# VectorE takes over the sums and low parts of the stored hidden blocks in a two-layer decoder

## The chip, the core and the metric

The kernel runs on one core of one Trainium2 chip. The metric is the time of one execution on the device, in microseconds; every time below is in that unit unless it says ns. The kernel before takes 2506.91 (median of three runs, 2505.78 to 2507.61).

A core has five engines, each with an instruction queue of its own that it works off in order: TensorE (PE; its weight loads are PEld), VectorE (DVE), ScalarE (ACT), GpSimd (POOL) and SyncE (SP). SP issues most loads, ACT the stores spoken of here. Engines wait for each other by semaphores.

## The reference

Two decoder layers over x of 1024 x 1024 (sequence by channels), all in float32. The part that the change touches is the first half of the feed-forward layer:

```python
def swiglu_ffn(x, w_gate, w_up, w_down):
    return (jax.nn.silu(x @ w_gate) * (x @ w_up)) @ w_down

for l in range(DEPTH):
    ...                       # mixer, cross-attention over memory, each with a LayerNorm
    y = swiglu_ffn(x, ffn_wg[l], ffn_wu[l], ffn_wd[l])
    x = layer_norm(ALPHA * x + y, ln_ffn_g[l], ln_ffn_b[l])
```

The hidden width is 2816, so x @ w_gate and x @ w_up are products of 1024 x 1024 by 1024 x 2816, and the last one is 1024 x 2816 by 2816 x 1024.

## The kernel before

**Products.** A float32 number is split into a high part (rounded to float32r) and a low part (the rest, also as float32r). A product of two such numbers is three matmuls of 128 x 128 by 128 x 512: low by high, high by low, high by high (lines 210 to 212). A large matrix product is made with seven block products in the place of eight (Strassen's scheme in Winograd's form): sums of blocks of both sides are formed first, and the results are added afterwards.

**The gate and up stage** (function ffn). The hidden columns are 22 blocks of 128; block c and block c + 11 form a pair, and so do the two halves of the sequence. For each c from 1 to 10 there are two steps m: an even m for the gate weights and an odd one for the up weights. Each step is seven block products, in the order 1, 2, 6, 5, 7, 3, 4 (ORDER_P); each product is 4 x 3 = 12 matmuls into a bank of PSUM named P. That is 140 products in a layer. c = 0 is done without the scheme ahead of them (plain, banks named pl).

Products 1, 6, 7 and 4 run one after another in one bank, 5 and 3 in a second, 2 in a third. After products 1, 6 and 5 ScalarE copies the bank to a tile u (line 1296); only then may the next product of that bank begin. After products 2, 7, 3 and 4 the result is finished (finish): for the gate VectorE adds u to the bank (line 1199) and ScalarE takes the SiLU (line 1200; product 4 directly from the bank, line 1197); for the up part VectorE adds (1206) and multiplies by the gate (1207; product 4 at once, 1204). The result lies in tiles hf.

**The weights' operands** (operands, operand). For each product a block of weights, or a sum of blocks, is split: ScalarE casts the high part (line 1112), VectorE subtracts for the low part (line 1113). The sums are s1 (line 1130), s2 (1133), a11 - a21 (1136) and a12 - s2 (1139), all on VectorE. Operands are made three products ahead: while product n is put in the queue, the operand of n + 3 is.

**The stored blocks** (store). When the four tiles of a block c are finished, its sums and differences s1 to s4 are made, each is split, and high and low parts go to DRAM (hD), from where the down stage loads them as its operands. GpSimd makes the four sums (lines 1180 to 1185) and the low parts (1167, 1171); ScalarE makes the high parts (1166, 1170) and issues the stores (1174). These steps are put in a list, later, each with a number of products to wait; emit_later, called once in each product, behind the product's matmuls and ahead of its copy or finish, puts those that are due into the queues.

**The down stage** (ffn_down) follows without a break; its products run in banks D. VectorE sums blocks of the down weights (line 777) and splits them (lines 215 and 216), and VectorE and GpSimd multiply and add a row of gains and offsets to the residual x (lines 1366 and 1367).

All of these tiles but the weights as loaded (raw, four buffers) lie in one pool of 44 pages; a page that comes free is given to a later tile, which waits for the page's last user.

## Time and profile before

| | |
|---|---|
| median of three runs | 2506.91 |
| the profiled execution | 2508.21 |
| its span, first to last instruction | 2506.4 |
| mean granted clock of TensorE | 0.974 |
| busy: PE / PEld | 2325.8 (93%) / 1916.3 (76%) |
| busy: DVE / ACT / POOL | 1826.7 (73%) / 1049.4 (42%) / 1027.0 (41%) |

The shares are of the whole span. Matmuls overlap in the pipeline, so the duration of one (some 395 ns) is longer than the distance from one to the next. In a timeline a row is one instruction, or several of a kind without idle time between them, with its start and duration; the bracket at its end is the idle time of the engine just before it and what ended that. A group's row gives the count, the busy time, the mean duration in ns, and the idle time before its instructions. P, D, u, op, hf, s, sh, x and wp in such rows are the tiles named above (sh: a high part on its way to DRAM; sg: a gate; op: an operand of weights).

### The profile page before, as it was taken

The numbers are of one execution on the slowest core, as the hardware profiler recorded it, in microseconds if no ns is written. First come the engines' busy times: TensorE is split into PE (matmuls) and PEld (weight loads), VectorE is DVE, ScalarE is ACT, GpSimd is POOL, SyncE is SP. The second block draws the span as 40 slices with busy tenths as digits, with TensorE's granted clock in tenths as the row PEclk, the third lists the DMA queues.
The fourth block names the chain that finished last, engine by engine and source line by source line (L and its number), as shares of the span: only waits on it lengthen the run. The fifth ranks groups of instructions, "written<-read, shape, count | busy, mean of one in ns | idle before, by whom it ended". The sixth has DMA issues, their size and how long they took to land. (4 is left out here: it accounts for less than half of the span.)

```text
span 2506.4 us, 29564 instructions
## 1 busy us (share of the span) xinstructions
PE 2325.8 (93%) x11208; PEld 1916.3 (76%) x11208; DVE 1826.7 (73%) x1950; ACT 1049.4 (42%) x1727; POOL 1027.0 (41%) x577
## 2 busy tenths in 40 slices
PE   8999997798979999999999989797999999999997
PEld 7777776696868777777778789686787777777886
DVE  6986788787895777777784556879666767677555
ACT  3254554354637443434312244455563434342212
POOL 1333446666472434343530074656523525255001
PEclk9999998898989999999999999899999999999999
DMA  4211133150212243434786642302114344349773
GB/s 181 67 34 35 34 118 126 34 185 17 88 39 93 101 160 118 167 111 173 280 339 238 228 152 97 106 18 109 51 57 171 120 157 138 140 160 357 292 282 118
DMA packets 117341, 344.02 MB, mean 137 GB/s; under 512 B 10832, under 2 KB 11344, under 8 KB 117200
## 3 DMA queue, kind: packets, MB, share of 16 engines
q1 hardware_dynamic: 70560, 244.35, 28.0%
q10 hardware_dynamic: 46640, 97.79, 10.3%
q8 instruction: 89, 1.46, 0.2%
q14 instruction: 52, 0.43, 0.1%
HBM read 239.34 MB, written 102.76 MB: 136 GB/s over the span
## 5 line engine op out<-in xcount | busy, mean ns | idle before, releaser
L210 PE MATMUL P<-xh,op 128*128 128x512 f32 x1120 | 442.6, 395 | 40.4 <-ACT u L1296 37.7
L211 PE MATMUL P<-xl,op 128*128 128x512 f32 x1120 | 438.7, 392 | 0.0
L212 PE MATMUL P<-xh,op 128*128 128x512 f32 x1120 | 438.5, 392 | 0.0
L1113 DVE TENSOR_TENSOR op<-raw,op 128x512 fp32r<-128x512 f32 x200 | 231.0, 1158 | 154.6 <-ACT op L1112 103.3
L210 PEld LDWEIGHTS P<-xh,op 128*128 128x128 f32 x1120 | 211.8, 189 | 99.0 <-ACT u L1296 47.0
L210 PE MATMUL D<-dh,dl 128*128 128x512 f32 x560 | 226.0, 404 | 58.3 <-DVE x L247 35.4
L210 PE MATMUL D<-dh,wp 128*128 128x512 f32 x616 | 241.6, 392 | 10.4 <-ACT dh L215 9.2
L1180 POOL TENSOR_TENSOR s<-hf,hf 128x512 f32<-128x512 f32 x22 | 34.8, 1584 | 524.6 <-DVE hf L1207 439.3
L211 PE MATMUL D<-dl,wp 128*128 128x512 f32 x616 | 241.8, 392 | 5.2 <-DVE dl L216 5.1
L212 PEld LDWEIGHTS P<-xh,op 128*128 128x128 f32 x1120 | 211.8, 189 | 45.0
L211 PEld LDWEIGHTS P<-xl,op 128*128 128x128 f32 x1120 | 211.7, 189 | 43.1
L211 PE MATMUL D<-dl,dh 128*128 128x512 f32 x560 | 224.5, 401 | 21.1 <-DVE dl L216 21.1
L212 PE MATMUL D<-dh,wp 128*128 128x512 f32 x616 | 240.7, 391 | 0.0
L125 POOL TENSOR_TENSOR wl<-raw,wh 128x1024 fp32r<-128x1024 f32 x64 | 172.4, 2705 | 166.0 <-ACT wh L123 165.7
L216 DVE TENSOR_TENSOR dl<-wp,dh 128x1024 fp32r<-128x1024 f32 x96 | 142.5, 1493 | 117.8 <-ACT dh L215 75.6
L212 PE MATMUL D<-dh,dh 128*128 128x512 f32 x560 | 223.5, 399 | 0.0
L257 POOL TENSOR_SCALAR lst<-lst 128x1 f32<-128x1 f32 x48 | 27.3, 568 | 460.2 <-ACT sq L256 459.8
L215 ACT CAST dh<-wp 128x1024 fp32r<-128x1024 f32 x96 | 93.7, 989 | 266.5 <-DVE wp L777 68.6
L365 DVE SCALAR_TENSOR_TENSOR cacc<-sig,par,cacc 128x1023 f32<-128x1023 f32 (+14 forms) x120 | 175.6, 1464 | 2.5
L210 PEld LDWEIGHTS D<-dh,dl 128*128 128x128 f32 x560 | 108.9, 195 | 85.4 <-issue 36.6
L1112 ACT CAST op<-raw 128x512 fp32r<-128x512 f32 x200 | 121.9, 620 | 104.6 <-DVE raw L1139 73.2
L216 POOL TENSOR_TENSOR dl<-xf,dh 128x1024 fp32r<-128x1024 f32 x48 | 141.5, 2964 | 39.6 <-ACT dh L215 29.2
(272 smaller groups left out, 5498.2 us busy)
## 6 DMA issues: line engine op xcount, KB each, us to landing
wp<-hD SPq DMA_DIRECT2D x140, 512.0 KB, 5.8
hD<-sh ACTq DMA_DIRECT2D x66, 512.0 KB, 5.2
raw<-in_wg SPq DMA_DIRECT2D x44, 512.0 KB, 4.4
raw<-in_wu SPq DMA_DIRECT2D x44, 512.0 KB, 3.8
hD<-hf ACTq DMA_DIRECT2D x44, 512.0 KB, 5.8
hD<-s ACTq DMA_DIRECT2D x44, 512.0 KB, 3.6
wp<-in_wd SPq DMA_DIRECT2D x40, 512.0 KB, 7.7
xD<-x ACTq DMA_DIRECT2D x32, 512.0 KB, 3.8
```

The source lines that it names most:

```text
L125: eng.tensor_tensor(lo, raw, hi.bitcast(F32), op=ALU.subtract)
L210: mm(out, ll, rh, start=start, stop=False, skip_group_check=more)
L211: mm(out, lh, rl, start=False, stop=False, skip_group_check=more)
L212: mm(out, lh, rh, start=False, stop=stop, skip_group_check=more)
L215: self.nc.scalar.copy(hi, src)
L216: getattr(self.nc, lo_engine).tensor_tensor(lo, src, hi.bitcast(F32), op=ALU.subtract)
L257: nc.gpsimd.tensor_scalar(st[:, 3:4], st[:, 3:4], 1.0 / D, LN_EPS, op0=ALU.mult, op1=ALU.add)
L365: nc.vector.scalar_tensor_tensor(acc[:, s:], u[:, :S - s], w[:, j:j + 1], acc[:, s:], op0=ALU.mult, op1=ALU.add)
L1112: nc.scalar.copy(pg[:, 0], src)
L1113: getattr(nc, lo_engine).tensor_tensor(pg[:, 1], src, pg[:, 0].bitcast(F32), op=ALU.subtract)
L1180: gp(s1, a21, a22, op=ALU.add)
```

## The change

The four sums and the low parts of a stored block move from GpSimd to VectorE. They are laid out in eight steps, one in each of the eight products after the block is finished: the first four products take two sums, two sums, the low part of two blocks, and the low part of a11; the next two the low parts of the sums; the stores of the sums' parts come in the last two. The casts on ScalarE and the stores stay on ScalarE, in a new order. For the last block of a layer the steps fall in groups of three, three and two on the next three calls of emit_later. In operands a weights' sum is put into VectorE's queue one product earlier: while the operand of one product is made, the sum that the following product needs is made first.

```diff
--- before.py
+++ after.py
@@ -1139,9 +1139,10 @@
                     eng(a12, a12, s2, op=ALU.subtract)
 
             src = {1: a11, 2: a12, 3: a12, 4: a22, 5: s1, 6: s2, 7: a21}
-            for j in order:
-                if j in (3, 5, 6, 7):
-                    need({3: 4, 5: 1, 6: 2, 7: 3}[j])
+
+            for j, after in zip(order, order[1:] + (None,)):
+                if after in (3, 5, 6, 7):
+                    need({3: 4, 5: 1, 6: 2, 7: 3}[after])
                 yield operand(src[j], lo_engine)
 
         def product(bank, w, x, first):
@@ -1156,38 +1157,42 @@
             a11, a21, a12, a22 = h[0][:, 0, :], h[0][:, 1, :], h[1][:, 0, :], h[1][:, 1, :]
             s12, s34 = self.page("s12", [2, 512]), self.page("s34", [2, 512])
             s1, s2, s3, s4 = s12[:, 0, :], s12[:, 1, :], s34[:, 0, :], s34[:, 1, :]
-            gp = nc.gpsimd.tensor_tensor
             dst = self.hD[c // 2][:, :, :, c % 2, :]
             last = c == HF - 1
             part = {}
 
-            def split(k, src):
+            def high(k, src):
                 part[k] = self.page("sh", [2, 512], F32R)
                 nc.scalar.copy(part[k], src)
-                gp(src.bitcast(F32R), src, part[k].bitcast(F32), op=ALU.subtract)
-
-            def split11():
-                nc.scalar.copy(a21.bitcast(F32R), a11)
-                gp(a11.bitcast(F32R), a11, a21, op=ALU.subtract)
+
+            def low(k, src):
+                tt(src.bitcast(F32R), src, part[k].bitcast(F32), op=ALU.subtract)
 
             def put(to, src):
                 nc.scalar.dma_start(to.rearrange("s p n -> p s n"), src.bitcast(F32))
 
-            def put2(k, lo, src):
-                put(dst[1, lo:lo + 2], part.pop(k))
-                later.append((2, lambda: put(dst[0, lo:lo + 2], src)))
-
-            gp(s1, a21, a22, op=ALU.add)
-            gp(s3, a11, a21, op=ALU.subtract)
-            gp(s2, s1, a11, op=ALU.subtract)
-            if last:
-                split11()
-            gp(s4, a12, s2, op=ALU.subtract)
-            n = (0, 1, 0, 1, 1, 2, 2) if last else (0, 1, 1, 2, 3, 3, 4)
-            for at, f in zip(n, (lambda: split(1, h[1]), lambda: put2(1, 1, h[1]),
-                                 lambda: (last or split11(), later.append((0 if last else 3, lambda: put(dst[:, 0], h[0])))),
-                                 lambda: split(3, s12), lambda: split(5, s34), lambda: put2(3, 3, s12), lambda: put2(5, 5, s34))):
-                later.append((at, f))
+            def put_high(k):
+                put(dst[1, k:k + 2], part.pop(k))
+
+            def sums(i):
+                if i == 0:
+                    tt(s1, a21, a22, op=ALU.add)
+                    tt(s3, a11, a21, op=ALU.subtract)
+                else:
+                    tt(s2, s1, a11, op=ALU.subtract)
+                    tt(s4, a12, s2, op=ALU.subtract)
+
+
+            steps = ((lambda: sums(0), lambda: high(1, h[1])),
+                     (lambda: sums(1),),
+                     (lambda: nc.scalar.copy(a21.bitcast(F32R), a11), lambda: low(1, h[1])),
+                     (lambda: tt(a11.bitcast(F32R), a11, a21, op=ALU.subtract), lambda: put_high(1), lambda: high(3, s12)),
+                     (lambda: low(3, s12), lambda: high(5, s34)),
+                     (lambda: put(dst[0, 1:3], h[1]), lambda: put(dst[:, 0], h[0]), lambda: low(5, s34)),
+                     (lambda: put_high(3), lambda: put(dst[0, 3:5], s12)),
+                     (lambda: put_high(5), lambda: put(dst[0, 5:7], s34)))
+            for n, fs in enumerate(steps):
+                later.extend((n // 3 if last else n, f) for f in fs)
 
         def finish(m, st, i, j, add, bank):
```

What this does to the queues is shown at three places. The first is VectorE's queue from the end of a stored block of the first layer (c = 3, tiles hf_7357 and hf_7358; s_1132 and s_1133 hold its sums) through the first products of the next gate. Before:

```order
L1113 TENSOR_TENSOR op_7493<-s_7434,op_7493 128x512
L1136 TENSOR_TENSOR raw_7293<-raw_7144,raw_7293 128x512
L1113 TENSOR_TENSOR op_7517<-raw_7293,op_7517 128x512
L1199 TENSOR_TENSOR sg_7496<-P_1141_7520,u_7514 128x512
L1139 TENSOR_TENSOR raw_7144<-raw_7144,s_7434 128x512
L1113 TENSOR_TENSOR op_7539<-raw_7144,op_7539 128x512
L1113 TENSOR_TENSOR op_7559<-raw_7293,op_7559 128x512
L1113 TENSOR_TENSOR op_7586<-raw_7295,op_7586 128x512
L1199 TENSOR_TENSOR sg_7497<-P_1137_7498,u_7579 128x512
L1113 TENSOR_TENSOR op_7605<-raw_7295,op_7605 128x512
L1199 TENSOR_TENSOR sg_7496<-P_1146_7562,u_7557 128x512
```

After, from the same place on (the finishing multiplication of the block's last product stands just before it in both):

```order
L1136 TENSOR_TENSOR raw_7288<-raw_7144,raw_7288 128x512
L1113 TENSOR_TENSOR op_7490<-s_7434,op_7490 128x512
L1179 TENSOR_TENSOR s_1132_7487<-hf_7357,hf_7358 128x512
L1180 TENSOR_TENSOR s_1133_7488<-hf_7357 128x512
L1139 TENSOR_TENSOR raw_7144<-raw_7144,s_7434 128x512
L1113 TENSOR_TENSOR op_7515<-raw_7288,op_7515 128x512
L1182 TENSOR_TENSOR s_1132_7487<-s_1132_7487,hf_7357 128x512
L1183 TENSOR_TENSOR s_1133_7488<-hf_7358,s_1132_7487 128x512
L1204 TENSOR_TENSOR sg_7493<-P_1141_7518,u_7512 128x512
L1113 TENSOR_TENSOR op_7535<-raw_7144,op_7535 128x512
L1169 TENSOR_TENSOR hf_7358<-hf_7358,sh_7510 128x1024
L1113 TENSOR_TENSOR op_7554<-raw_7288,op_7554 128x512
```

The sums of the weights (L1136, L1139) stand one operand earlier, the block's sums (L1179 to L1183) and low parts (L1169, L1189) stand between the operands' low parts (L1113), and the addition for the gate (L1199 before, L1204 after) behind them.

The second is ScalarE's queue over the same products. Before:

```order
L1112 CAST op_7493<-s_7434 128x512
L1166 CAST sh_7511<-hf_7358 128x1024
L1296 COPY u_7514<-P_1137_7498 128x512
L1112 CAST op_7517<-raw_7293 128x512
L1174 DMA hD_74<-sh_7511 128x2x512
L1170 CAST hf_7357<-hf_7357 128x512
L1200 ACTIVATE sg_7496<-sg_7496 128x512
L1112 CAST op_7539<-raw_7144 128x512
L1166 CAST sh_7554<-s_1132_7487 128x1024
L1296 COPY u_7557<-P_1137_7498 128x512
```

After:

```order
L1112 CAST op_7490<-s_7434 128x512
L1166 CAST sh_7510<-hf_7358 128x1024
L1301 COPY u_7512<-P_1137_7495 128x512
L1112 CAST op_7515<-raw_7288 128x512
L1205 ACTIVATE sg_7493<-sg_7493 128x512
L1112 CAST op_7535<-raw_7144 128x512
L1188 CAST hf_7357<-hf_7357 128x512
L1301 COPY u_7552<-P_1137_7495 128x512
L1112 CAST op_7554<-raw_7288 128x512
L1172 DMA hD_74<-sh_7510 128x2x512
L1166 CAST sh_7572<-s_1132_7487 128x1024
L1301 COPY u_7574<-P_1145_7557 128x512
```

The cast for the high part of hf_7358 stays in front of the first copy u; the cast for s_1132 moves from in front of the second copy to behind it, ahead of the third; the cast for s_1133, which stood ahead of the third copy, comes behind it; and the stores (DMA) come later.

The third is VectorE's queue at the end of the stage, from the last finishing multiplication on (the last block's tiles are hf_9373 and hf_9374, its sums s_1400 and s_1401; dl and wp belong to the down stage). Before:

```order
L1204 TENSOR_TENSOR hf_9374<-P_1381_9375,sg_9225 128x512
L216 TENSOR_TENSOR dl_9545<-wp_1397_9500,dh_9544 128x1024
L216 TENSOR_TENSOR dl_9555<-wp_1421_9542,dh_9554 128x1024
L216 TENSOR_TENSOR dl_9601<-wp_1426_9552,dh_9600 128x1024
L1366 TENSOR_TENSOR x_9526<-x_9526,lng_9530 128x1024
L1367 TENSOR_TENSOR x_9526<-x_9526,lnb_9531 128x1024
L216 TENSOR_TENSOR dl_9645<-wp_1435_9598,dh_9644 128x512
```

After:

```order
L1209 TENSOR_TENSOR hf_9374<-P_1381_9375,sg_9222 128x512
L1179 TENSOR_TENSOR s_1400_9507<-hf_9373,hf_9374 128x512
L1180 TENSOR_TENSOR s_1401_9508<-hf_9373 128x512
L1182 TENSOR_TENSOR s_1400_9507<-s_1400_9507,hf_9373 128x512
L1183 TENSOR_TENSOR s_1401_9508<-hf_9374,s_1400_9507 128x512
L1169 TENSOR_TENSOR hf_9374<-hf_9374,sh_9519 128x1024
L216 TENSOR_TENSOR dl_9544<-wp_1397_9500,dh_9543 128x1024
L216 TENSOR_TENSOR dl_9554<-wp_1421_9541,dh_9553 128x1024
L1189 TENSOR_TENSOR hf_9373<-hf_9373 128x512
L1169 TENSOR_TENSOR s_1400_9507<-s_1400_9507,sh_9583 128x1024
L1169 TENSOR_TENSOR s_1401_9508<-s_1401_9508,sh_9586 128x1024
L216 TENSOR_TENSOR dl_9602<-wp_1426_9551,dh_9601 128x1024
```

The last block's eight instructions, which stood in GpSimd's queue, now stand ahead of the down stage's first splits and among them, and ahead of the row multiplications (L1366 before, L1371 after).

## Rows read from the trace of the kernel before

**Rows 1.** Whole program: line engine op out<-in xcount | busy, mean ns | idle before.
```profile
L210 PE MATMUL P<-xh,op 128*128 128x512 f32 x1120 | 442.6, 395 | 40.4 <-ACT u L1296 37.7
...
L1113 DVE TENSOR_TENSOR op<-raw,op 128x512 fp32r<-128x512 f32 x200 | 231.0, 1158 | 154.6 <-ACT op L1112 103.3
```

**Rows 2.** Windows of both gate and up stages: busy us (count) by engine, clock, DMA, GB/s.
```profile
827.00:1237.00 410.00, 389.84 (x1683) 316.40 (x1682) 294.32 (x322) 171.40 (x281) 163.18 (x81) 0.99 0.44 154
1864.80:2274.50 409.70, 389.45 (x1681) 316.21 (x1680) 293.98 (x321) 171.49 (x281) 163.11 (x81) 0.99 0.44 154
```

**Rows 3.** By tile, P and D: duration ns min/median/max, first and last start us.
```profile
L210 PE MATMUL P<-xh,op x560: 389/389/750, 827.2 to 1236.3; 128*128 128x512 f32 x187
...
L210 PE MATMUL D<-dh,wp x81: 389/389/792, 1237.0 to 1299.7; 128*128 128x512 f32 x81
```

**Rows 4.** Timeline of TensorE: start us, us, what [idle before <-releaser].
```profile
834.07 0.50 PE L210 MATMUL P<-xh,op 128*128 128x512 f32 x1 [1.24 <-ACT u L1296]
...
949.83 0.39 PE L211 MATMUL P<-xl,op 128*128 128x512 f32 x1
...
960.94 0.39 PE L212 MATMUL P<-xh,op 128*128 128x512 f32 x1
963.22 0.50 PE L210 MATMUL P<-xh,op 128*128 128x512 f32 x1 [1.90 <-ACT u L1296]
```

**Rows 5.** Timeline of GpSimd around the same wait.
```profile
949.41 1.52 POOL L1180 TENSOR_TENSOR s<-hf,hf 128x512 f32<-128x512 f32 x1 [22.23 <-DVE hf L1207]
...
962.76 5.20 POOL L1167 TENSOR_TENSOR s<-s,sh 128x1024 fp32r<-128x1024 f32 x2 [2.22 <-ACT sh L1166]
```

**Rows 6.** Timeline of VectorE.
```profile
831.77 0.68 DVE L1204 TENSOR_TENSOR hf<-pl,sg 128x512 f32<-128x512 f32 x1
...
953.10 0.68 DVE L1204 TENSOR_TENSOR hf<-P,sg 128x512 f32<-128x512 f32 x1
...
957.26 2.12 DVE L1113 TENSOR_TENSOR op<-raw,op 128x512 fp32r<-128x512 f32 x1 [0.69 <-ACT op L1112]
...
970.32 0.69 DVE L1113 TENSOR_TENSOR op<-raw,op 128x512 fp32r<-128x512 f32 x1 [1.21 <-ACT op L1112]
970.93 0.68 DVE L1199 TENSOR_TENSOR sg<-P,u 128x512 f32<-128x512 f32 x1
```

**Rows 7.** Timeline of ScalarE.
```profile
960.02 0.63 ACT L1200 ACTIVATE sg<-sg 128x512 f32<-128x512 f32 x1 [2.27 <-DVE sg L1199]
961.12 0.62 ACT L1112 CAST op<-raw 128x512 fp32r<-128x512 f32 x1 [0.47 <-DVE raw L1139]
961.65 1.04 ACT L1166 CAST sh<-s 128x1024 fp32r<-128x1024 f32 x1
962.59 0.58 ACT L1296 COPY u<-P 128x512 f32<-128x512 f32 x1
```

**Rows 8.** Windows at three places of a layer, columns as in Rows 2.
```profile
878.50:886.00 7.50, 5.59 (x18) 4.32 (x18) 5.62 (x4) 4.49 (x7) 5.16 (x2) 0.77 0.71 215
955.00:965.00 10.00, 8.10 (x36) 6.34 (x36) 7.37 (x6) 6.05 (x10) 7.70 (x4) 1.00 0.30 81
1300.00:1400.00 100.00, 100.00 (x443) 82.81 (x442) 50.53 (x61) 20.79 (x21) 0.00 (x0) 1.00 0.75 271
```

**Rows 9.** Groups by form: VectorE's low parts of 1024 columns.
```profile
L216 DVE TENSOR_TENSOR xl<-xf,xh 128x1024 fp32r<-128x1024 f32 x32 | 37.6, 1222 | 6.8 <-ACT xh L215 6.6
```

**Rows 10.** End of the stage: timelines of TensorE and VectorE, and GpSimd's group.
```profile
1271.65 0.79 PE L210 MATMUL D<-dh,wp 128*128 128x512 f32 x1 [4.59 <-ACT dh L215]
...
1274.40 0.63 PE L212 MATMUL D<-dh,wp 128*128 128x512 f32 x1
1274.83 0.63 PE L210 MATMUL D<-dh,wp 128*128 128x512 f32 x1
...
1267.11 3.36 DVE L777 TENSOR_TENSOR wp<-wp,wp 128x1024 f32<-128x1024 f32 x1
...
L1366 POOL TENSOR_TENSOR x<-x,lng 128x1024 f32<-128x1024 f32 x6 | 19.1, 3184 | 0.0
```

## The prediction, made before the changed kernel was run

> **What bounds the kernel now.** I read the groups of the whole program first, then the windows and the first and last matmuls of the two gate and up stages, then the timelines of TensorE, GpSimd, VectorE and ScalarE around one stall there. The groups show that TensorE's idle time in the stage's products (P) is 40 us and that it waits mostly for ScalarE's copy u, and that VectorE's subtraction for the low parts takes 1158 ns on average [rows 1]. The windows show TensorE busy for 389.8 of 410 us with VectorE at 294 and GpSimd at 163, in both layers alike [rows 2]. So the stage is TensorE's, and what can be won is what TensorE loses in it. That is counted so: from 949.83 to 960.94 lie 49 matmuls without a gap, 0.2267 each [rows 4]; 140 products of 12 are 1680 matmuls, 380.8 us; the stage runs from 827.2 to 1237.0 [rows 3], 409.8. **Lost: 28.9 us a layer**, 57.8 in both.
>
> Where: one pattern returns in each pair of gate and up, nine times a layer. At 963.22 TensorE has waited 1.90 for u [rows 4]. The copy ran only at 962.59, behind a cast of a block's sums (1.04), a cast that had waited 0.47 for VectorE's sum L1139, and at 960.02 the SiLU of a product that was long done, which had waited 2.27 for VectorE [rows 7]. ScalarE is late because VectorE is, and VectorE is late while GpSimd works on the stored block, from 949.41 to about 968 [rows 5]. In that stretch a 512-column VectorE instruction with both inputs in SBUF takes up to 2.12, while one that reads PSUM takes 0.68 in the midst of it, and after 968 the same subtraction takes 0.69 and the next starts 0.61 later [rows 6]. With the restart and a second small wait two products later, such a place costs about 2.65 by the starts of the matmuls; at two places a layer the granted clock falls too (0.77 over 7.5 us against 1.00 around another such wait [rows 8]), and the place costs 3.8. The first pair loses 2.2 in two such waits, the first ending at 834.07 [rows 4].
>
> **The change part by part.** *GpSimd loses all its work in the stage*: 8 instructions for each of 11 blocks a layer, 163 us [rows 2]. Nothing waits behind it there. What goes is the slowing of VectorE.
>
> By the Trainium skill (SBUF — State Buffer, section "SBUF: two separate sides") the port pair that GpSimd shares with VectorE is an exclusive lock, and a VectorE instruction with two SBUF inputs that meets a GpSimd one waits for all of it. The 2.12 against 0.69, and the 0.68 of the instruction that reads PSUM, agree [rows 6]. The rule speaks against the change at the end of the stage, where GpSimd has other work and VectorE's eight new instructions with two SBUF inputs meet it: by it that end comes to its bad bound (below), and the whole to 2461.
>
> *VectorE gains 8 instructions a block*: four sums and the low part of a11 at 0.61 start to start, three low parts of 1024 columns at 1.22 [rows 6, 9], 6.7 us. They fall on seven products of the gate half. There VectorE has 7 operand low parts, 4 weight sums, 5 block steps of 512 and 3 finishing instructions: 19 x 0.61 = 11.6, and 3 x 1.22 = 3.7, together 15.3 in the 7 x 2.72 = 19.0 us that TensorE needs (16.8 with 0.69 for 0.61). So it fits, if no product's share comes late. I walked the seven in the new order, counted from the end of the block's last product, with a product's result readable 0.3 after its end (an estimate: a matmul is out 0.39 after its start, which is 0.16 into the next slot [rows 4]):
> - product 1: VectorE finishes the block at 0.95, then four instructions to 3.4; ScalarE copies u1 from 3.0 to 3.6, wanted at 5.4 by the product that reuses the bank.
> - product 2: VectorE's four to 6.0, the gate's addition to 6.6, SiLU to 7.2.
> - product 6: two casts to 8.2, u6 from 8.5 to 9.0, wanted at 10.9. This is the copy that stalls now. VectorE is at 9.6.
> - product 5: u5 from 11.2 to 11.7, wanted at 13.6; VectorE to 10.8.
> - product 7: VectorE's low parts to 14.1, the addition on the bank to 14.7, wanted at 16.3.
> - products 3 and 4: VectorE to 18.4 and 20.3. Operands are made 3 products ahead and come 4 or more us early.
>
> The least slack is 1.6 us, so the nine waits go, and nothing takes their place in the walk. The up half carries 18 VectorE instructions, 11 to 12.4 us, and has no wait now.
>
> *The weights' sums a product ahead*: no instruction more. ScalarE's cast then finds its sum made, which saves the 0.47 of rows 7 in front of u6. What the moved sum delays on VectorE is one low part by 0.6 to 1.2, of an operand with 4 us to spare: nothing, and without that cover 0.6.
>
> *The order of casts and stores on ScalarE*: the same casts; the first is still ahead of u1, the one for s12 now follows u6 and stands before u5. The stores of the high parts of the sums leave 3 products later, those of the low parts at most one later; in the walk they find their data made 2 us or more before.
>
> *The first pair* keeps its loss. VectorE ends the last unmixed product's multiplication at 831.77 [rows 6], the first cast follows it, and u1 follows the cast as before: 2.2 a layer stays.
>
> Sum for the stage: 28.9 - 2.2 = 26.7 a layer, 53.4. In it are 3.2 us a layer for the two drops of the clock. Both lie at such a wait, and 100 us in which TensorE is never idle run at 1.00 [rows 8]. If the drops stayed, the stage would give 47.0.
>
> The Trainium skill (TensorE: Matmul & The Clock Gate, "What's actually happening") has it that the clock is throttled unless activity releases it. The drops at the waits agree. By it the 3.2 goes with the waits; a drop that came with the load would stay.
>
> *The end of the stage.* The first product of the down stage that needs a sum of blocks waits 4.59, and then for its low part, and goes on at half the clock (1.2 of 2.4 GHz), 0.43 a matmul [rows 10]; from the starts of the matmuls this costs 8.3 a layer against 0.2267 each. It waits for L777 on VectorE, done at 1270.5; TensorE was there at 1267.06, and a cast and a low part, 2.3, come between, so 1264.7 would have done. VectorE's queue up to L777 has after the change 8 block instructions (6.7), three splits (3.7), four row multiplications and additions (4.9), a short split and L777 (1.8): 17.1 from 1237.9 is 1255 alone. GpSimd still has its own six row instructions there, 3.2 each [rows 10], 19.2, while its block work, which stood before them, is gone, so that they start earlier. Beside one, VectorE's 1024 columns take 3.36, not 1.22 [rows 10], and it loses 0.64 of that time. The bounds: none met, 1255; all six met and VectorE stopped for all of it, 1274.2, which is 3.7 later than now and would leave 53.4 - 7.4, or 2461 in all. With a third of them before 1237.9 (an estimate: the first of GpSimd's three tensors is loaded ahead of the others) and the rest met at 0.64: 17.1 + 8.2, 1263.2, with the block's first store some 4 us later than now and the loads behind it too. I take 5 of the 8.3, between the end without a wait and a wait cut in half: 10 in both layers.
>
> **Sum.** 53.4 + 10 = 63.4. The profiled execution took 2508.2, 1.8 more than its span and 1.3 more than the median of the runs. 2508.2 - 63.4 - 1.3 = 2443.5, say **2444**.
>
> **The rivals.**
> *All of it goes*, the end of the stage too: 2 x (28.9 + 8.3) = 74.4, less the first pairs 4.4: 2437; even these gone, 2433. For it: the walk to 1263.2. This is within the forecast's own range, 2433 to 2461 (the bad bound at the end of the stage).
>
> *Half of it stays.* ScalarE has one queue; casts of 1.05 stand before u1 and u5, and a SiLU that waits for VectorE stands before u6. If VectorE lags by some 3 us in product 2, where it has five instructions, u6 is late again: nine waits of 1.3 and the drops of the clock stay, 11.7 + 3.2 a layer, and the end gives nothing. 2 x (26.7 - 14.9) = 23.6: 2483. Against it: 1.9 us of slack at u6.
>
> *Nothing comes of it*: the wait moves to another copy or to the stores on ScalarE, or the end of the stage gives back what the stage won; 2502 to 2512. Little speaks for it, since TensorE has 20 us of idle time a layer [rows 2] and the next stage starts relative to this one's end.
>
> *VectorE becomes the bound, slower.* If its instructions kept their average of 1158 [rows 1], for instance because DMA or ScalarE and not GpSimd slowed them, the gate half would take 16 x 1.158 + 3 x 2.05 + 3 x 0.68 = 26.7, the up half 14 x 1.158 + 4 x 0.68 = 18.9: 45.6 a pair where it is 40.8 now. 20 x 4.8 = 96: 2603. It decides from 0.80 a 512-column instruction on (16 x 0.80 + 3 x 1.42 + 2 = 19.0). Against it: 0.69 as soon as GpSimd stops, with the same casts and loads going on [rows 6].
>
> **How the numbers follow.** Forecast with the first rival 0.74, half of it 0.12, nothing 0.05, VectorE the bound 0.09. A measurement of this kernel tells 0.2%, 5 us, from no change. Faster: 0.74 + 0.12 = 0.86; same 0.05; slower 0.09. The range leaves out the last two cases, which hold 0.14: from 2431, just under the first rival with all gone, to 2484, the second.
>
> **What would show it.** Right: GpSimd at zero through the stage; VectorE's L1113 near 0.69 and its busy time there near 300 us; TensorE's idle time on P from 40 to some 4 us, what is left in the first pair; the stage near 383 us in each layer; no clock below 1.00 inside it; the wait before D shorter than 4.59. Wrong in a step: waits for u at the same product (half stays); L1113 over 0.8 with GpSimd idle (VectorE the bound); a longer wait for L777 (the end).

## The result, and the profile after

The changed kernel takes 2452.14 (median of four runs, 2451.46 to 2453.01) against 2506.89 for the kernel before on the same chip: a ratio of 0.9782, 95% interval 0.9765 to 0.9799. Its profiled execution took 2451.65, its span is 2449.9, its mean granted clock 0.976. The forecast was 2444 with a range of 2431 to 2484: faster, inside the range, 8 too low.

The page after, busy times first and then two groups, in the columns of [rows 1]:

```profile
PE 2312.4 (94%) x11208; PEld 1916.5 (78%) x11208; DVE 1778.0 (73%) x2126; ACT 1044.2 (43%) x1727; POOL 665.9 (27%) x401
...
L210 PE MATMUL P<-xh,op 128*128 128x512 f32 x1120 | 436.2, 389 | 2.1 <-ACT u L1301 2.1
...
L1113 DVE TENSOR_TENSOR op<-raw,op 128x512 fp32r<-128x512 f32 x200 | 137.9, 689 | 147.5 <-ACT op L1112 147.5
```

TensorE's idle time in front of P went from 40.4 to 2.1 and VectorE's low part from 1158 to 689 ns [rows 1]. GpSimd does 361 us less; VectorE, with eight instructions a block more, is busy for 49 us less. Both stages, in the columns of [rows 2]:

```profile
827.00:1212.00 385.00, 383.94 (x1693) 317.27 (x1692) 276.54 (x403) 169.50 (x282) 2.06 (x1) 1.00 0.46 166
1837.00:2222.00 385.00, 383.94 (x1693) 317.27 (x1692) 276.49 (x404) 170.48 (x284) 1.63 (x1) 1.00 0.47 166
```

The clock is 1.00 through the stage, and GpSimd's one instruction there belongs to the down stage. The first P product starts at 826.32 and the first D product at 1208.78: 382.45 where it was 409.75 [rows 3]; the second layer gives 382.47. What is lost against 380.8 lies in two waits of the first pair. In the other pairs the prediction's walk can be laid beside ScalarE's copies u1, u6 and u5 behind the block that ends at 942.22 (c = 3, one slot of 0.23 behind its last matmul's start at 941.99):

```profile
945.13 0.59 ACT L1301 COPY u<-P 128x512 f32<-128x512 f32 x1 [0.94 <-PE P L212]
...
950.58 0.59 ACT L1301 COPY u<-P 128x512 f32<-128x512 f32 x1
...
953.29 0.59 ACT L1301 COPY u<-P 128x512 f32<-128x512 f32 x1 [0.66 <-PE P L212]
```

They start 2.9, 8.4 and 11.1 after that end; the walk had 3.0, 8.5 and 11.2. At the end of the stage the wait for the first sum of down weights is nearly as long as before [rows 10]. Timeline of TensorE after:

```profile
832.57 0.50 PE L210 MATMUL P<-xh,op 128*128 128x512 f32 x1 [0.65 <-ACT u L1301]
...
1243.00 0.80 PE L210 MATMUL D<-dh,wp 128*128 128x512 f32 x1 [4.14 <-ACT dh L215]
1244.26 0.80 PE L211 MATMUL D<-dl,wp 128*128 128x512 f32 x1 [0.47 <-DVE dl L216]
```

So the stage gave 2 x 27.3 = 54.6. In the first 60 us of the down stage the matmuls lost 8.29 and 8.34 before and 7.46 and 7.61 after, counted by their starts against 0.2267 each: 1.6. Together 56.2, and the profiled executions differ by 56.6.

### The profile page after: what moved, and what is told of

Its sections match the earlier page's. It is cut to its first block, busy times and chain, and to the rows that moved or that the text cites. A ratio compares the mean times of both kernels' runs of the same rounds, so it can differ in the third digit from the quotient of the medians.

```text
span 2449.9 us, 29443 instructions
## 1 busy us (share of the span) xinstructions
PE 2312.4 (94%) x11208; PEld 1916.5 (78%) x11208; DVE 1778.0 (73%) x2126; ACT 1044.2 (43%) x1727; POOL 665.9 (27%) x401
## 3 DMA queue, kind: packets, MB, share of 16 engines
q10 hardware_dynamic: 46640, 97.79, 11.1%
## 5 line engine op out<-in xcount | busy, mean ns | idle before, releaser
L210 PE MATMUL P<-xh,op 128*128 128x512 f32 x1120 | 436.2, 389 | 2.1 <-ACT u L1301 2.1
L212 PE MATMUL P<-xh,op 128*128 128x512 f32 x1120 | 435.7, 389 | 0.0
L1371 POOL TENSOR_TENSOR x<-x,lng 128x1024 f32<-128x1024 f32 x6 | 17.9, 2980 | 867.8 <-DVE s L1179 421.4
L1113 DVE TENSOR_TENSOR op<-raw,op 128x512 fp32r<-128x512 f32 x200 | 137.9, 689 | 147.5 <-ACT op L1112 147.5
L216 DVE TENSOR_TENSOR dl<-wp,dh 128x1024 fp32r<-128x1024 f32 x96 | 127.6, 1336 | 115.9 <-ACT dh L215 72.8
L257 POOL TENSOR_SCALAR lst<-lst 128x1 f32<-128x1 f32 x48 | 27.3, 568 | 466.7 <-ACT sq L256 466.3
L216 DVE TENSOR_TENSOR dl<-B,dh 128x1024 fp32r<-128x1024 f32 x48 | 117.9, 2488 | 40.7 <-ACT dh L215 40.7
```

The source lines that it names most:

```text
L210: mm(out, ll, rh, start=start, stop=False, skip_group_check=more)
L212: mm(out, lh, rh, start=False, stop=stop, skip_group_check=more)
L216: getattr(self.nc, lo_engine).tensor_tensor(lo, src, hi.bitcast(F32), op=ALU.subtract)
L257: nc.gpsimd.tensor_scalar(st[:, 3:4], st[:, 3:4], 1.0 / D, LN_EPS, op0=ALU.mult, op1=ALU.add)
L1113: getattr(nc, lo_engine).tensor_tensor(pg[:, 1], src, pg[:, 0].bitcast(F32), op=ALU.subtract)
L1371: eng.tensor_tensor(x[t], x[t], gx[0], op=ALU.mult)
```

## The experiments

"Stage" below is the time from the first P to the first D matmul of the first layer; without any wait it is 380.8. "Down loss" is the loss in the first 60 us of the down stage, both layers.

### The two halves of the change, each alone

*e1_store_alone*: the stored blocks on VectorE, the weights' sums where they were.

```diff
-            for j, after in zip(order, order[1:] + (None,)):
-                if after in (3, 5, 6, 7):
-                    need({3: 4, 5: 1, 6: 2, 7: 3}[after])
+            for j in order:
+                if j in (3, 5, 6, 7):
+                    need({3: 4, 5: 1, 6: 2, 7: 3}[j])
```

> The stored blocks' sums and low parts are on VectorE in eight steps, the weights' sums stand where they stood before the change. Theory (GpSimd's work stretches VectorE's instructions with two SBUF inputs, and so made ScalarE's copy u late): nearly all of the gain, 2450 to 2458, TensorE idle on P 2 to 8 us, L1113 at 0.69. Rival (the weights' sums a product ahead removed ScalarE's wait in front of u): most of the gain missing, 2480 to 2505, the waits for u at product 7 still there.

Measured: 2456.56, ratio 0.9800 (0.9785 to 0.9814); stage 383.43, so this half alone gives 26.3 of the 27.3; L1113 at 691 ns. The theory's numbers.

*e2_sums_alone*: the kernel before with the weights' sums a product ahead, and nothing else.

```diff
-            for j in order:
-                if j in (3, 5, 6, 7):
-                    need({3: 4, 5: 1, 6: 2, 7: 3}[j])
+            for j, after in zip(order, order[1:] + (None,)):
+                if after in (3, 5, 6, 7):
+                    need({3: 4, 5: 1, 6: 2, 7: 3}[after])
```

> Only the weights' sums stand a product ahead; GpSimd still makes the stored blocks' sums and low parts as before. Theory (GpSimd beside VectorE): little, 2495 to 2508, since the saved wait is 0.5 us at each of nine places a layer and VectorE's instructions stay at some 1160 ns; TensorE idle on P 30 to 42 us. Rival (the sums ahead): 2455 to 2480, idle on P under 15 us.

Measured: 2456.96, ratio 0.9805 (0.9789 to 0.9822); stage 384.25. This went against my theory: GpSimd still works 166.7 us in the stage and L1113 still takes 964 ns, yet the nine waits are gone, and this half alone gives 25.5 of the 27.3. The page of e2_sums_alone:

```profile
L210 PE MATMUL P<-xh,op 128*128 128x512 f32 x1120 | 436.4, 390 | 5.0 <-ACT u L1296 4.4 <-DVE sg L1199 0.6
...
L1113 DVE TENSOR_TENSOR op<-raw,op 128x512 fp32r<-128x512 f32 x200 | 192.6, 964 | 148.7 <-ACT op L1112 136.5 <-issue 12.2
```

Either half alone is worth about 50 of the 55, so the gains do not add. The reason lies just ahead of the place that the prediction read. TensorE and VectorE of the kernel before, at the end of the same stored block:

```profile
950.06 0.39 PE L212 MATMUL P<-xh,op 128*128 128x512 f32 x1
...
949.82 1.66 DVE L1133 TENSOR_TENSOR s<-s,raw 128x512 f32<-128x512 f32 x1
952.17 1.01 DVE L1113 TENSOR_TENSOR op<-s,op 128x512 fp32r<-128x512 f32 x1 [0.69 <-ACT op L1112]
```

950.06 is the start of the block's last matmul. VectorE's next instruction after these is the block's finish at 953.10 [rows 6], 3.04 later. In front of it stand the next gate's sum s2 (L1133), VectorE's own wait of 0.69 while ScalarE casts that sum, and its low part; and GpSimd, which starts on the block at 949.41 [rows 5], makes the sum and the low part longer. In the changed kernel the finish follows the matmul by 0.43:

```profile
941.99 0.39 PE L212 MATMUL P<-xh,op 128*128 128x512 f32 x1
...
942.42 0.69 DVE L1209 TENSOR_TENSOR hf<-P,sg 128x512 f32<-128x512 f32 x1 [0.16 <-PE P L212]
```

Over the nine blocks of the first layer this distance is 3.04 to 3.10 before, 1.75 in e1_store_alone, 0.43 in e2_sums_alone and after. With the sums ahead, L1133 and its cast are through one product earlier, before GpSimd starts. VectorE and GpSimd of e2_sums_alone:

```profile
940.00 0.69 DVE L1133 TENSOR_TENSOR s<-s,raw 128x512 f32<-128x512 f32 x1
...
943.38 0.69 DVE L1204 TENSOR_TENSOR hf<-P,sg 128x512 f32<-128x512 f32 x1 [0.16 <-PE P L212]
...
946.55 1.78 DVE L1139 TENSOR_TENSOR raw<-raw,s 128x512 f32<-128x512 f32 x1
...
942.85 1.52 POOL L1180 TENSOR_TENSOR s<-hf,hf 128x512 f32<-128x512 f32 x1 [21.30 <-DVE hf L1207]
```

GpSimd stretches VectorE here as much as before (1.78 for L1139), and the slack after the finish takes it up.

### GpSimd's work, with either order of the sums

*e3_steps_on_gpsimd*: the changed kernel, but the eight steps of a block run on GpSimd. *e7_steps_on_gpsimd_sums_old*: the same with the diff of e1_store_alone as well.

```diff
-                tt(src.bitcast(F32R), src, part[k].bitcast(F32), op=ALU.subtract)
+                gp(src.bitcast(F32R), src, part[k].bitcast(F32), op=ALU.subtract)
...
-                    tt(s1, a21, a22, op=ALU.add)
+                    gp(s1, a21, a22, op=ALU.add)
```

> The changed kernel, its eight steps and its order of casts and stores, but GpSimd makes the sums and low parts in these steps. Theory (the engine matters): GpSimd's 18 us a block stand beside VectorE again, L1113 over 1.0, waits for u come back in part since the work is spread over seven products: 2475 to 2510. Rival (the new schedule matters, not the engine): 2450 to 2458, idle on P under 5 us with GpSimd at some 160 us in the stage.

Measured: 2457.81, ratio 0.9806 (0.9791 to 0.9821); stage 384.27, although L1113 takes 1024 ns: the rival's numbers.

> GpSimd makes the stored blocks' sums and low parts in the eight steps, and the weights' sums stand where they stood before the change: of the change only the new steps are left. Theory now (the waits need two things together, VectorE stretched by GpSimd and the cast that waits for its sum just made, and either one's removal is enough): the waits for u come back, 2485 to 2515. Rival (spreading the block's work over eight products is enough by itself): 2452 to 2465.

Measured: 2484.57, ratio 0.9910 (0.9896 to 0.9923); stage 395.82; the theory's numbers, but for 0.4. The finish is again 3.05 late, in VectorE's rows as in the kernel before:

```profile
945.62 0.39 PE L212 MATMUL P<-xh,op 128*128 128x512 f32 x1
...
945.38 1.67 DVE L1133 TENSOR_TENSOR s<-s,raw 128x512 f32<-128x512 f32 x1
947.73 1.01 DVE L1113 TENSOR_TENSOR op<-s,op 128x512 fp32r<-128x512 f32 x1 [0.69 <-ACT op L1112]
948.67 0.68 DVE L1210 TENSOR_TENSOR hf<-P,sg 128x512 f32<-128x512 f32 x1
...
957.92 0.50 PE L210 MATMUL P<-xh,op 128*128 128x512 f32 x1 [1.04 <-ACT u L1302]
```

The wait for u stays at the same product, and a pair loses 1.33 by the starts in place of 2.7. So the two runs that differ in the sums alone are 11.6 apart in the stage: with GpSimd's work in place the order of the sums decides. This kernel also shows a third part of the change. It has GpSimd's work and the old place of the sums, as the kernel before, and the finish is as late, but its stage is 13.9 shorter (395.82 against 409.75). That is worth half of the gain, and it comes from the new steps alone, which spread the block's work over eight products and reorder casts and stores; no run parts the two.

*e4_gpsimd_beside*: the changed kernel with eleven subtractions of 512 columns on a scratch tile more, for each block, on GpSimd.

```diff
+            z = self.sq.bitcast(F32)
+            for _ in range(11):
+                nc.gpsimd.tensor_tensor(z, z, z, op=ALU.subtract)
```

> The changed kernel, and GpSimd gets at each stored block 11 subtractions of 512 columns on a scratch tile that nobody reads, some 18 us as before; nothing waits for them in the stage. Theory: VectorE's instructions are stretched as before although it waits for nothing of GpSimd, and it has more of them now: waits for u come back, 2490 to 2560, L1113 over 1.0, the granted clock below 1.00 at some of the waits. Rival (what GpSimd does in its own tiles doesn't matter, only what waits for it): 2450 to 2456, L1113 at 0.69.

Measured: 2556.15, ratio 1.0199 (1.0183 to 1.0214). They wait for nothing and ran in one piece from 787.7 to 973.6, from ahead of the stage on, and not beside each block, so the run does not repeat the load of the kernel before. Windows of the stage's start and of its rest:

```profile
830.00:990.00 160.00, 124.62 (x486) 98.28 (x487) 147.40 (x124) 51.43 (x86) 136.13 (x96) 0.89 0.31 109
990.00:1260.00 270.00, 270.00 (x1193) 223.57 (x1192) 192.41 (x284) 117.43 (x196) 0.00 (x0) 1.00 0.46 166
```

GpSimd at work without a break takes the stage from the changed kernel (TensorE idle 35 of 160, VectorE 92% busy), and nothing is lost behind its end. GpSimd's work can cost TensorE time, then, but in the kernel before it needed the sums in front of the finish.

### The first pair

*e5_first_plane_first*: for the last block of a layer the sums that read a11, its low part and its store come at once, in `store` itself. *e6_first_block_later*: the same, and the steps of a layer's first block start one product later:

```diff
+            if last:
+                sums(0)
+                tt(s2, s1, a11, op=ALU.subtract)
+                nc.scalar.copy(a21.bitcast(F32R), a11)
+                tt(a11.bitcast(F32R), a11, a21, op=ALU.subtract)
+                high(1, h[1])
+                put(dst[:, 0], h[0])
+                ...
-                later.extend((n, f) for f in fs)
+                later.extend((n + (c == 0), f) for f in fs)
```

(The last two lines are e6's alone.)

> The changed kernel, but for the last block of a layer the sums that read a11, the low part of a11 and the store of its plane stand right behind the block, ahead of the other parts. Theory (at the end of the stage SyncE's queue of loads stands behind the store of that plane, and VectorE waits 4.4 us for a load that is issued too late): that store leaves 3 to 5 us earlier, so do the loads behind it, TensorE's wait before the first product with a sum goes from 4.3 + 1.0 to 0 to 2.5 us a layer: 2443 to 2449. Rival (the loads are late since the DMA engines are full): 2450 to 2453, the wait as it was.

Measured: 2464.00, ratio 0.9828 (0.9814 to 0.9841), slower than the changed kernel; down loss 13.82 and 13.40 (discussed below).

> The kernel with the first plane stored first, and besides all eight steps of a layer's first block come one product later, so that no cast for a stored block stands in front of the layer's first copy u. Theory (that copy waits behind the cast, which waits for a late multiplication on VectorE): the 1.6 us of the first pair go to 0 to 0.7 a layer, 2 to 3 us less than without it: 2440 to 2447. Rival (VectorE's late work itself is what product 6 waits for, or the steps meet worse one product later): no change against the kernel without it, or up to 3 us more.

Measured: 2458.74, ratio 0.9811 (0.9797 to 0.9824); stage 380.80 in both layers, no matmul waits. Against e5 5.3 less, 3.3 by the stage.

*e8_first_block_later_alone*: the changed kernel with that shift and no other edit.

```diff
-                later.extend((n // 3 if last else n, f) for f in fs)
+                later.extend((n // 3 if last else n + (c == 0), f) for f in fs)
```

> The changed kernel with one edit: the eight steps of a layer's first block start one product later. The theory (the two losses of the changed kernel's first pair, 0.92 and 0.69 us a layer, come from VectorE having the first block's steps and the first products' finishes at once) expects the gate and up stage at 380.8 us in each layer instead of 382.5, and a time of 2447 to 2450. The rival (the shift changes which load or store waits behind which at the stage's end, and loses there what it gains) expects 2452 or more, with the loss in the first products of the down stage.

Measured: 2444.63 (2444.18 to 2449.16), ratio 0.9756 (0.9743 to 0.9770); stage 380.80 in both layers, down loss 8.49 and 8.54. Of the versions that compute the whole result it had the lowest time, below both expected ranges. That the stage has no loss left is shown; that the whole is 7.5 below the changed kernel, where the stage gives 3.3, lies within the scatter of the runs (the two intervals overlap), and its down stage is no better.

### The end of the stage

In the changed kernel VectorE stands idle in front of L777; the load it waits for was issued late, since SP stood behind a store. VectorE, SP, ScalarE's queue and GpSimd after:

```profile
1210.18 2.89 DVE L1180 TENSOR_TENSOR s<-hf 128x512 f32<-128x512 f32 x1
1213.00 2.89 DVE L1182 TENSOR_TENSOR s<-s,hf 128x512 f32<-128x512 f32 x1
...
1220.13 0.69 DVE L1189 TENSOR_TENSOR hf<-hf 128x512 fp32r<-128x512 f32 x1
...
1240.13 1.41 DVE L777 TENSOR_TENSOR wp<-wp,wp 128x1024 f32<-128x1024 f32 x1 [4.36 <-DMA wp<-in_wd]
...
1211.12 2.88 SPq L1366 DMA_DIRECT2D x<-xD  x2
1225.06 0.81 SPq L96 DMA_DIRECT2D wp<-hD  x2
...
1232.42 0.41 SPq L96 DMA_DIRECT2D wp<-in_wd  x1
...
1217.98 3.29 ACTq L1172 DMA_DIRECT2D hD<-hf  x2
...
1209.94 2.59 POOL L1371 TENSOR_TENSOR x<-x,lng 128x1024 f32<-128x1024 f32 x1 [420.87 <-DMA lng<-in_ln_xa_g]
```

SP's load of the last block (1225.06) waits for that block's store to land; the store waits for L1189, which is queued behind the sums, and GpSimd's rows (L1371) stretch these. The store is the second of the row 1217.98; it left at 1220.9, 12.1 after the stage's end. The load for L777 (1232.42) left 23.6 after that end, before 16.8 (1253.82 against 1237.0). That was the theory; a second one came from the DMA share.

The theory covers half of these 6.8. SP stood at this load in the kernel before, too, and went on 13.0 after the stage's end (1249.99), now 16.3: 3.3 later. The other 3.5 arise behind that load. What differs there is the number of stores ahead of the load for L777. In the kernel before, three of the last block's seven came behind it; now all seven, 512 KB each, come ahead of it. That load and the last three stores before (first three rows), and the last store after:

```profile
1253.82 0.33 SPq L96 DMA_DIRECT2D wp<-in_wd  x1
...
1270.63 0.37 ACTq L1174 DMA_DIRECT2D hD<-hf  x1
...
1277.45 0.92 ACTq L1174 DMA_DIRECT2D hD<-s  x2
...
1230.67 0.37 ACTq L1172 DMA_DIRECT2D hD<-s  x1
```

At the 410 GB/s of the windows below, three such stores take 3.8 (an estimate). No run held them back, so their part is not shown.

*e9_first_plane_sooner*: e8, and for the last block the low part of a11 right behind the sums, its store ahead of that of h[1], the block's second tile.

```diff
+            if last:
+                steps = ((lambda: sums(0), lambda: high(1, h[1]), lambda: nc.scalar.copy(a21.bitcast(F32R), a11),
+                          lambda: tt(s2, s1, a11, op=ALU.subtract),
+                          lambda: tt(a11.bitcast(F32R), a11, a21, op=ALU.subtract),
+                          lambda: tt(s4, a12, s2, op=ALU.subtract), lambda: low(1, h[1])), (), (),
+                         ...
+                         (lambda: put(dst[:, 0], h[0]), lambda: put(dst[0, 1:3], h[1]), lambda: low(5, s34)),
+                         steps[6], steps[7])
```

> The kernel with the first block's steps one product later, and for a layer's last block the first plane's low part made right behind the sums, ahead of the low part of h1 and of the two down splits; its store stands ahead of h1's in the same call, all other stores and loads where they were in the program. The theory (the load of the down stage's first packed weights is issued late because SP's queue stands behind that store, which waits for the low part) expects the store some 3 us earlier, the load behind it too, and the first wait with a sum in the down stage at 1.5 to 3.5 us instead of 4.3: 2440 to 2446. The rival (the load waits for another transfer's landing, not for that store's issue) expects no gain in the down stage: 2447 to 2455.

Measured: 2446.64, ratio 0.9759 (0.9746 to 0.9773). The store left 8.5 after the stage's end, in the changed kernel 12.1, but SP went on only 0.4 sooner (15.9 after that end for 16.3), since the store took 7.3 to land where it took 4.1; down loss 8.36 and 6.89. The time lies between the two ranges. In the first layer the rival held (8.36 against e8's 8.49); the second gained 1.65. The DMA engines are full there, in the kernel before as well. The windows ahead of and behind the stage's end, of the kernel before and then of after:

```profile
1217.00:1237.00 20.00, 20.00 (x90) 16.54 (x89) 12.89 (x18) 7.68 (x12) 0.99 (x1) 1.00 0.92 347
1237.00:1241.00 4.00, 4.00 (x19) 3.34 (x18) 0.70 (x2) 1.56 (x3) 3.92 (x4) 1.00 1.03 410
```

```profile
1188.80:1208.80 20.00, 20.00 (x90) 16.54 (x89) 11.12 (x16) 7.36 (x12) 0.00 (x0) 1.00 0.98 367
1208.80:1212.80 4.00, 4.00 (x19) 3.34 (x18) 3.83 (x4) 1.06 (x1) 2.78 (x2) 1.00 1.03 409
```

*e10_no_x_loads* takes bytes away, *e11_no_wait_for_store* the standing queue (both on e8). Neither computes the whole result. The first two lines are e10's, without its edit of the row multiplication; the last three are e11's:

```diff
-                    nc.sync.dma_start(x[t], self.xD[t])
+                    nc.sync.dma_start(x[t][:, 0:32], self.xD[t][:, 0:32])
...
-                        w.add(h[part, DOWN_A[j]], ...)
+                        src = h[part, DOWN_A[j]] if (j, g) != (1, 5) else self.hD[0][part, DOWN_A[j], :, 0:1]
+                        w.add(src, ...)
```

> The kernel with the first block's steps one product later (e8), and of the eight tiles of x that the down stage loads back (512 KB each) only 32 of 1024 columns; the row multiplication reads the row of gains twice in x's place, so the number of instructions and of loads stays and the residual x is left out of the result. New theory of the end of the stage: the 16 DMA engines are full from 20 us before the down stage begins until its first product with a sum (share 0.98 to 1.03, 367 to 420 GB/s in the changed kernel), so the load that L777 waits for comes when the bytes ahead of it are through, whatever VectorE and the queues do. Four of these loads, 2.1 MB or 5.1 us at 410 GB/s, stand ahead of it and two behind. It expects the wait of 4.3 to 4.8 at 0 to 1.5, and 2433 to 2439. The rival (SP's queue stands behind the landing of the last block's store, and that sets when the load is issued) expects the wait at 3.5 or more, and 2442 to 2447.

Measured: 2444.11, ratio 0.9749 (0.9734 to 0.9763); the wait 3.77 and 3.39 by the starts, down loss 6.44 and 6.16: the rival's numbers. With the bytes gone the engines are not full from 1211 to 1223 (shares of 0.75, 0.36 and 0.16 in the three windows); behind that, when SP goes on, they are again (0.90 to 1.08). SP's longest wait, the emptiest window, and VectorE in front of L777:

```profile
SPq L96 <- DMA hD<-hf: 15.5, 1, 15.5
```

```profile
1219.00:1223.00 4.00, 4.00 (x19) 3.30 (x19) 4.00 (x3) 1.06 (x1) 1.83 (x1) 1.00 0.16 60
```

```profile
1233.24 3.42 DVE L1371 TENSOR_TENSOR x<-lng 128x1024 f32<-128x1024 f32 x1
...
1237.83 1.22 DVE L777 TENSOR_TENSOR wp<-wp,wp 128x1024 f32<-128x1024 f32 x1
```

SP stood 4.5 longer than after. It came to that load 3.3 sooner, and it went on 1.2 later, since GpSimd's rows met L1189 (2.88 for 0.69) and the splits ahead of it, and the store left later. L777 itself no longer waits for a load (no bracket): VectorE's rows end last there, one of them stretched to 3.42. They are late because the split ahead of them waited 4.65 for ScalarE's cast of a load that SP had sent late.

> The same kernel (e8), but the last group's operand of the first down product is loaded from the first block's place in DRAM in place of the last block's, so that no load of that product waits for the last block's stores; as many bytes and loads as before, and the result of that product wrong in one block. The theory of full DMA engines expects that SP no longer stands for 11 us but the load of the weights lands at most 2 us sooner, because the bytes ahead of it are the same: wait 2.5 to 4.5, 2441 to 2446. The rival (the standing queue) expects the load to be issued up to 10 us sooner and to land in time: the wait at 0 to 1, 2432 to 2438.

Measured: 2441.81, ratio 0.9739 (0.9722 to 0.9755); the wait 2.31 and 2.25, down loss 5.23 and 5.70. SP no longer stands for 11, and the engines stay full (1.02 to 1.05 in each window to 1241). But SP still stands 5.4 at the load for L777 itself (1232.09), until a store of a high part has landed. At L777 of this run VectorE, whose rows GpSimd stretches, and the load come almost together:

```profile
1232.09 0.33 SPq L96 DMA_DIRECT2D wp<-in_wd  x1
...
1234.41 3.30 DVE L1372 TENSOR_TENSOR x<-x,lnb 128x1024 f32<-128x1024 f32 x1
1237.97 1.23 DVE L777 TENSOR_TENSOR wp<-wp,wp 128x1024 f32<-128x1024 f32 x1 [0.26 <-DMA wp<-in_wd]
```

So neither theory alone: there are three limits close together (the bytes, SP behind the stores, VectorE beside GpSimd's rows). Taking one away shortens e8's wait of 4.7 by 1.0 (e10) or 2.4 (e11), and then the next one holds. Which share each has in the changed kernel stays open.

*e12_x_later* tries to ease all three: four of the eight tiles of x loaded later, their rows in the second down product.

```diff
-            if j == 1 and g < 4:
-                for t in (g, g + 4):
+            t = {(1, 0): 0, (1, 1): 1, (1, 2): 2, (1, 3): 3, (1, 5): 4, (5, 0): 5, (5, 1): 6, (5, 2): 7}.get((j, g))
...
+          (1, 5): ((3, "vector"),), (5, 1): ((4, "gpsimd"),), (5, 2): ((5, "gpsimd"),), (5, 3): ((6, "gpsimd"),),
+          (5, 4): ((7, "vector"),)}
```

> The kernel with the first block's steps one product later (e8), and the second four of the eight tiles of x are loaded back later, one in each of four operands from the last of the first down product on, with their row multiplications in the second down product (three on GpSimd, one on VectorE); nothing is left out. The theory as the last two runs left it (three limits stand close together behind the stage: full DMA engines, SP's queue behind the last block's store, and VectorE beside GpSimd's rows) expects all three to ease: no GpSimd work beside the last block's sums and low parts, so the store some 4 us sooner, 1 MB or 2.6 us fewer loads ahead of the load for L777, and VectorE's rows at 1.22. The wait of 4.5 to 4.8 goes to 0 to 2, and the time to 2433 to 2440. The rival (the loads and rows are only moved, and meet the second product's sums and low parts on VectorE, or add to a full stretch there) expects new waits in the second product and 2443 to 2455.

Measured: 2455.32, ratio 0.9791 (0.9778 to 0.9804), down loss 11.22 and 11.75. The first wait is gone (no gap over 1.03 there), and the rival came in its place: GpSimd's rows meet the second product's sums. GpSimd, VectorE and TensorE there:

```profile
1248.92 3.23 POOL L1374 TENSOR_TENSOR x<-x,lnb 128x1024 f32<-128x1024 f32 x1
...
1249.85 3.38 DVE L778 TENSOR_TENSOR wp<-wp,wp 128x1024 f32<-128x1024 f32 x1
...
1254.42 0.50 PE L211 MATMUL D<-dh,wp 128*128 128x512 f32 x1 [3.36 <-ACT dh L216]
```

e5 failed in a fourth way. Its store left at 1216.79, 7.7 after its stage's end (12.1 in the changed kernel), but SP stood 13.9 at a load of weights, which needs no stored data:

```profile
1216.79 0.37 ACTq L1172 DMA_DIRECT2D hD<-hf  x1
...
1204.05 1.62 SPq L96 DMA_DIRECT2D wp<-hD  x2
1219.61 0.33 SPq L96 DMA_DIRECT2D wp<-in_wd  x1
```

In the compiled program a DMA's landing raises one of eight counters, taken in turn in program order, and a DMA waits for the one before it on its own counter. The store's new place in the program put this load behind it: it left at 1219.61, when the store had landed. That is read from the waits, and no run tested it apart. The 5.4 at the load for L777 in e11 reads the same way: that load and the store it waited for use the same counter.

## Why the prediction was right, and where it was wrong

**The stage: right in size.** Forecast 53.4, measured 54.6. The nine waits and both drops of the clock went, and the walk held within 0.2: in it the gate's sums were already in the new order. Of the first pair's 2.2, which was to stay, 1.65 stayed. The right size does not confirm the cause: since either half of the change alone removes nearly all, the sum came out whichever half it was credited to.

**The cause: half wrong.** The step "the weights' sums a product ahead ... saves the 0.47" was mis-sized; alone it takes 25.5 us a layer out of the stage (409.75 to 384.25). The prediction looked for the start of the delay at GpSimd's start, 949.41, and read the finish at 953.10 only for its length of 0.68; against the matmul at 950.06 it was 2.6 later already than in the changed kernel, and the [0.69 <-ACT op L1112] in [rows 6] is the same pattern, one sum later. The wait needed two conditions: VectorE waits for ScalarE's cast of a sum in front of the finish, and GpSimd stretches what stands around it. Each half of the change removes one. How long the wait is depends on the block's steps besides: e7_steps_on_gpsimd_sums_old keeps both conditions, and its stage loses 15.0 where the kernel before loses 28.9.

**The end of the stage: the failed step.** Of 10 forecast, 1.6 came. The step took VectorE's queue up to L777 as the only limit. VectorE was indeed free early (done with the rows at 1235.8, and idle for 4.36), but then L777 waited for its load, which left 6.8 later after the stage's end than before. VectorE's new work had put off the store behind it on ScalarE, which left 12.1 after that end where it had left 6.3, and SP behind that store by 3.3. The other 3.5 arise at full DMA engines, with three stores more ahead of the load; how the causes share it stays open. The prediction named the later store and loads and then gave them no price; the DMA share there (0.92 and 1.03) was to be read in the trace of before.

**The rest.** Of the 8.6 between 2443.5 and 2452.1, 1.8 is the scatter of the profiled executions: I took off 1.3 from before's, and after's lies 0.5 below its median. "Half of it stays" did not come, nor did VectorE become the bound: 689 ns with GpSimd idle. Two numbers of the working were off without deciding the sum: by its own prices of a place, 3.8 and 2.65, the two drops of the clock cost 2.3 a layer and not 3.2, so that 48.8 and not 47.0 would be left if they stayed; and 831.77 is the start of the last unmixed multiplication, which ends at 832.45.

The rule of the Trainium skill that the prediction weighed (SBUF — State Buffer, section "SBUF: two separate sides": a VectorE instruction with two SBUF inputs waits for all of a GpSimd one that it meets) agrees with the rows after: L1180 from 1210.18 ends some 0.5 after GpSimd's instruction from 1209.94 to 1212.53 does. These waits did not set the end of the stage by VectorE's queue, as the prediction's bad bound had it; they put off the store.

## What to carry to other kernels

To find where a late engine became late, compare each of its finishing instructions with the end of the matmul it reads, and go back until one is on time. An operand chain that goes from one engine to another and back (sum, cast, low part) leaves a hole in the first engine's queue; make its first link a step earlier before moving work between engines. When work moves ahead of a store, price the chain store, landing, loads behind it, count the stores that come ahead of the next load, and read the DMA share of that stretch first.

## What the hardware showed

- GpSimd at work need not cost much: in e2_sums_alone it runs 166.7 us of a 384.2 stage and stretches L1113 to 964 ns, and the stage loses 3.4, all in the first pair (1.65 there without GpSimd's work).
- The granted clock fell where TensorE waited, though not at each wait (in the kernel before at two of nine places a layer): 1.00 in all of the changed kernel's stage, 0.89 over the stretch of e4_gpsimd_beside with TensorE idle for 35 of 160.
- With the DMA share at 1.03 some 410 GB/s move; there the store that e9_first_plane_sooner sent 3.6 sooner let SP go on 0.4 sooner.
